# New duration formulas for the kernel's own list scheduler, from the conv taps to the first FFN tiles

## The chip, the core and the metric

The kernel runs on one core of one Trainium2 chip. A core has five engines with queues of their own: TensorE (PE in the profile; its weight loads are listed apart as PEld), VectorE (DVE), ScalarE (ACT), GpSimd (POOL) and SyncE (SP), which here issues the DMA transfers. The metric is device time of one execution in microseconds (us), the median of several runs. Before the change three runs took 810.5, 808.39 and 804.48 us, median 808.39 us.

## The reference, cut to what matters

One decoder layer on 512 tokens of width 1024, in float32:

```python
z = rms_norm(x, mix_norm_g) @ w_in
(q, kc, vc, ks, vs, kw, vw, gl, zg, zc) = split(z)
y_nsa  = nsa_mixer(q, kc, vc, ks, vs, kw, vw, gl, ...)   # 8 heads of 64, 2 kv heads: compressed, selected
                                                        # and window branch, gated and summed
y_gmlp = gelu(u) * (tril(w_s) @ layer_norm(gelu(v)) + b) # width 256, chunks of 128 tokens, 4 groups
y_conv = silu(layer_norm(conv31(a * sigmoid(gate)) + b)) # width 256, causal depthwise, 31 taps
x = x + concat(rms_norm(y_nsa), rms_norm(y_gmlp), rms_norm(y_conv)) @ w_out
x = x + softmax((rms_norm(x) @ wq) @ (rms_norm(mem) @ wk).T / 16) @ (rms_norm(mem) @ wv) @ wo
                                                        # 4 heads of 256, mem has 256 tokens
h = conv3(rms_norm(x) @ w_up)                           # 2 x 2816
x = x + (silu(h[:, :2816]) * h[:, 2816:]) @ w_down
out = rms_norm(x)
```

With 512 tokens, 8 blocks of 64 and N_SELECT 16, the selected branch takes all blocks, and the window of 512 covers all earlier tokens. So both branches are causal attention over the whole sequence with keys and values of their own.

## The kernel before

Every large product is done in split precision. An operand is cut into a high part of type fp32r (on ACT) and the remainder (on DVE or POOL), and `mm3` issues three matmuls into one PSUM tile: high by high, high by low, low by high. Tiles are feature-major, 128 features by 512 tokens, eight k-steps for a sum over 1024.

The program has three stretches. The first norm and the first four column tiles of the input projection are written out by hand, and so is the FFN from its third tile on. All between is put in order, while the program is built, by the class `Lanes`, a list scheduler. Each piece of work is a Python generator (a lane). Before each step it yields the engine of the step, what it reads and which buffers it opens. `Lanes.start` works out when the step could start by a planned clock; `Lanes.run` finds for each engine the lane that can start first, takes among those within a margin EPS of it the most urgent one (smallest number in the table `prio`), and of these picks the earliest over all engines. The planned clock is advanced in `Lanes.account`, which the wrapper `Engine.__getattr__` calls for every instruction: an engine is busy for `cost`, and a reader on another engine may start LAT later, one on the same engine OWN later:

```python
LAT = {"E": 0.18, "S": 0.14, "V": 0.12, "G": 0.14, "D": 0.0}
OWN = {"E": 0.0, "S": 0.05, "V": 0.12, "G": 0.05, "D": 0.0}
```

E, S, V, G and D are TensorE, ScalarE, VectorE, GpSimd and the DMA queue. The plan sets only the order of the instructions in each queue; on the chip each engine takes its queue in order and waits with semaphores. All instructions carry the line of the wrapper, L186, so the rows are told apart by the names of tiles.

The lanes that the prediction speaks of, most urgent first among those that fill:

- `scores` multiplies, for 16 units (token block i of 4, kv head g of 2, branch b of 2; `units` in the order i, g, b), queries by keys of width 128(i+1). `soft` follows: a masked negated maximum per head on DVE (the fused reduce with the mask `cm`, listed as ISA or CUSTOM_DVE_ANT_0), an exponential with its sum on ACT, a reciprocal on DVE, a scaling by the gate on POOL.
- `turns` transposes the probabilities in blocks of 128 on PE, `mix` splits them (ACT, then DVE: tiles tB and tC) and multiplies by the values.
- `taps`: 30 dependent multiply-adds (`scalar_tensor_tensor`) for each of the two conv channel halves, 60 in all, on DVE, with 482 to 511 columns; their weights are the tile `cwh`. Their priority is 7.5, behind almost everything. `conv_post(i)` waits for both halves: two transposes of the accumulators on PE, a layer norm (BN_STATS first), tanh, a norm, and `put_back` into the concatenated y.
- `project` ends with the two halves of the gMLP's product, keys ("u", hf, c); gMLP's tail waits for the second half.
- `mem_work`, the filler of PE: 384 matmuls of 256 columns for keys ("mk") and values ("mv") of the cross-attention memory. `convert` splits its weights on ACT (tile whi) and on POOL (tile wlo, 64 pieces of 256 columns); all other weights are split on ACT and DVE.
- `pow_rstd` gives every norm its reciprocal root: a small operation on DVE and then a power on POOL (tile `nhalf`).
- `tiles("o", ...)`, the mixer's output projection, sums over the eight parts of y in the order in which they come, and ends the attention.

Of the kernel before, what the change touches and what calls it, by code (L numbers as in the profile page):

```python
# [41 lines left out]


class Lanes:
    """Puts the steps of concurrent generators in order: each generator yields the engine of its next step, what the
    step reads and the kinds of slots it opens; the step that can start first goes next, and among those of one
    engine that are about as early, the most urgent one."""

    LAT = {"E": 0.18, "S": 0.14, "V": 0.12, "G": 0.14, "D": 0.0}
    OWN = {"E": 0.0, "S": 0.05, "V": 0.12, "G": 0.05, "D": 0.0}  # L50
# [14 lines left out]
    def account(self, eng, name, a, k):  # L65
        args = list(a) + list(k.values())
        outs = [k["out"] if "out" in k else a[0]] + ([k["accum_out"]] if "accum_out" in k else [])
        aps = [x for x in args if isinstance(x, bass.AP)]
        n = max(int(np.prod(x.shape[1:])) for x in aps)
        if eng == "E":  # L70
            n = int(np.prod((a[2] if name == "matmul" else a[0]).shape[1:]))
            cost = max(int(np.prod(a[1].shape[1:])) / 1200, n / 2400)
        elif eng == "S":
            cost = 0.095 + n / 1200 + 0.093 * ("accum_out" in k)
            table = {AF.Gelu_apprx_tanh: 1, AF.Exp: 2, AF.Silu: 3}.get(a[2], self.table)
            if table != self.table:
                self.table = table
                cost += 1.28
        elif eng == "V":
            cost = (0.13 if name == "scalar_tensor_tensor" else 0.068) + n / 960  # L80
        elif eng == "G":
            cost = 0.245 + n / 1200 * (1 if name == "tensor_scalar" else 2)
        else:
            cost = 0.1 + n / 700
        start = max([self.free[eng]] + [self.at(eng, x) for x in aps] +
                    [self.rd.get(x.tensor.name, 0.0) for x in outs])
        if eng == "E":
            while start >= self.tick + self.TICK:
                self.warm = self.cols >= 3060
                self.cols, self.tick = 0.0, self.tick + self.TICK  # L90
            self.cols += n if name == "matmul" else 256
            cost *= 1 if self.warm else 2
        end = start + cost
        self.free[eng] = end
        if eng == "D":
            end += 2.0
        for x in aps if eng != "D" else ():
            self.rd[x.tensor.name] = max(self.rd.get(x.tensor.name, 0.0), end)
        for x in outs:
            self.wr[x.tensor.name] = (end, eng)  # L100
# [89 lines left out]
def body(ctx, tc, xT, memT, memN, cmask, cmaskT, w_a, w_v, w_u, w_c1, gains, smalls, ws_t, bcs, w_o, w_q, w_k, w_vm,  # L190
# [20 lines left out]
    def slab(shape=(P, T), dt=F32R):  # L211
        return psl.tile(list(shape), dt, name=nm("sl"), tag="slab", bufs=NSLAB)

    def tmp(tag, shape=(P, T), dt=F32):
        return ln.open(tag, pt.tile(list(shape), dt, name=nm("t" + tag), tag=tag, bufs=TB[tag]))
# [7 lines left out]
    def col(n):  # L223
        return pt.tile([P, n], F32, name=nm("rc"), tag="rcol", bufs=4)

    def ps(tag):
        return ln.open(tag, pp.tile([P, T], F32, name=nm("ps"), tag="bank", bufs=8))
# [12 lines left out]
    def mm3(o, ah, al, bh, bl, start, stop):  # L240
        E.matmul(o, ah, bh, start=start, stop=False)
        E.matmul(o, ah, bl, start=False, stop=False)
        E.matmul(o, al, bh, start=False, stop=stop)
# [10 lines left out]
        for _ in gen:  # L254
            pass

    # weight stream
    specs = [(("a", m), w_a[m], (8, 128)) for m in range(12)]
    specs += [(("c1", i), w_c1[i], (16, 64)) for i in range(2)]
    specs += [(("v", c), w_v[:, k0:k1, :], (k1 - k0, 280)) for c, (k0, k1) in enumerate(((0, 3), (3, 6), (6, 8)))]  # L260
# [9 lines left out]
    order = {s[0]: n for n, s in enumerate(specs)}  # L270
# [32 lines left out]
    def ahead(key, n=2):  # L303
        prep(order[key] + n)

    # constants
    gn = pc.tile([P, NGAIN], F32, name="gn")
    sm = pc.tile([P, NSMALL], F32, name="sm")
    cm = pc.tile([P, T], F32, name="cm")
# [1 line left out]
    def gv(name):  # L311
        a, b = GAIN[name]
        return gn[:, a:b]

    def sv(name):
        a, b = SMALL[name]
        return sm[:, a:b]
# [24 lines left out]
    class Norm:  # L342
        def __init__(self, gname):
            self.g = gv(gname)
            self.h = []
            self.acc = None
# [22 lines left out]
            mm3(o[:, :width], wh[:, k, :], wl[:, k, :], hi, lo, first and n == 0, last and n == len(ks) - 1)  # L369
            yield  # L370

    # start: first norm and the first two column tiles side by side
    n1 = Norm("g_mix")
    x = [slab(dt=F32) for _ in range(KD)]
    # wake the activation table and the tensor engine's clock while the first loads run
    wz = tmp("A")
    V.memset(wz, 0.0)
    S.activation(tiny([P, 4]), wz[:, 0:4], AF.Copy)
# [70 lines left out]
    wsr = slab(dt=F32)  # L449
    load(wsr, ws_t)  # L450

    # from here on lanes
    for tag, n in list(PB.items()) + list(TB.items()) + [("raw", NRAW), ("whi", NW), ("wlo", NW), ("bank", 8)]:
        ln.slots[tag] = [0.0] * n
    for o, tag in zip(zc, ("mm", "mm", "s", "s")):
# [14 lines left out]
    def pr(kind, j=0):  # L470
        return prio[kind][j]
# [32 lines left out]
    def spent(key):  # L504
        ln.done(*ready.pop(key))

    # depthwise convolution
    cw = pc.tile([P, 62], F32, name="cwh")
    V.tensor_scalar(cw, sv("cw"), 0.5, None, op0=ALU.mult)
    conv_acc = [slab(dt=F32) for _ in range(2)]  # L510
# [28 lines left out]
                                   op0=ALU.mult, op1=ALU.add)  # L539
        ln.mark(("taps", c), acc)  # L540

    # projection tiles
    qs, kh_, kl_ = {}, {}, {}

    def ev_cmp(kv, o):
# [139 lines left out]
                ln.add(pr("ev", 4), ev_u(hf, i, o))  # L685
        ln.mark("projected")

    # compressed blocks: second layer and scores of all tokens
    w2 = pc.tile([64, 2, 192], F32R, name="w2s")
    split(w2[:, 0, :], w2[:, 1, :], sv("w2")[0:64, :])  # L690
    vcz, kcz, sct = [], [], []
# [64 lines left out]
        for i in range(NT):  # L756
            ln.add(pr("cmp", i), compressed(i))

    # memory: statistics and parts, then keys and values as filler
    rm_col = col(2)  # L760
    rm_bc = pt.tile([P, MEM], F32, name="rm_bc", tag="rmbc", bufs=1)
    g_m = gv("g_m")
# [86 lines left out]
                ln.add(pr("memev", 1), mem_ev("mv", 2 * c + mt, o))  # L849
        ln.mark("quiet")  # L850

    # token-major tails of the gMLP and convolution groups
    g_out = gv("g_out")
    y_hi, y_lo = [None] * KD, [None] * KD
    gx = []
# [121 lines left out]
        yield from put_back(y, 6, i)  # L977
        ln.done(y)

    # native sparse attention  # L980
    units = [(i, g, b) for i in range(NT) for g in range(2) for b in range(2)]
    probs, left = {}, {}
    cmp_p, yts = {}, {}
# [187 lines left out]
                                   y_hi[kt][:, isl].bitcast(F32), op0=ALU.mult, op1=ALU.subtract)  # L1171
        ln.mark(("yn", i), *y_lo[:4])

    # projections of the residual stream
    def tiles(name, parts, deps, after, phases):
        """The first two tiles side by side, phase by phase of their sums, then one tile after the other."""
        o, count = {}, KD if name != "up" else 2
        jobs = [(m, k) for ks in phases for m in range(2) for k in ks]
        jobs += [(m, k) for m in range(2, count) for ks in phases for k in ks]
        first, last = phases[0][0], phases[-1][-1]  # L1180
        for m, k in jobs:
            key = (name, m)
            yield "E", [("w",) + key] + deps(k), ["mm"] if k == first else []
            if k == first:
                o[m] = ps("mm")
            wh, wl = ready[key]
            mm3(o[m], wh[:, k, :], wl[:, k, :], parts[0][k], parts[1][k], k == first, k == last)
            if k == last:
                spent(key)
                ln.add(pr("resid", ("o", "q", "ox", "up").index(name)), after(m, o[m]))  # L1190
# [39 lines left out]
        ln.done(o)  # L1230
        yield from pow_rstd(out_t, tot, 1.0 / D)

    # cross-attention
    n2, n3 = Norm("g_x"), Norm("g_f")
    rx, sc_col = col(NT), col(NT)
    xs, kp, vp = {}, {}, {}
# [108 lines left out]
        oh[k], ol[k] = hi, lo  # L1345
        ln.mark(("oh", k), hi, lo)

    # gated convolutional FFN
    rf = col(NT)
    rf_bc = pt.tile([P, T], F32, name="rf_bc", tag="rbc", bufs=1)  # L1350
    pending = []
# [12 lines left out]
        return iter(())  # L1364

    class Pairs:
        """The parts of a norm's tiles as two lists."""
        def __init__(self, norm, j):
            self.norm, self.j = norm, j

# [29 lines left out]
    lists = lambda norm: (Pairs(norm, 0), Pairs(norm, 1))  # L1400
# [12 lines left out]
    x = xs8  # L1413
    st_ = {}

    # gated convolutional FFN
    fw, fb = sv("fw"), sv("fb")
    ah, al = [], []
    st_["late"] = []
# [45 lines left out]
            split(ah[-1], al[-1], tv)  # L1465
            yield

    # down projection and final norm
    gfin = gv("g_fin")
    acc4 = pt.tile([P, T], F32, name="acc4", tag="acc", bufs=1)  # L1470

# [35 lines left out]
    for m in range(KD):  # L1507
        cuts = (slice(0, T),) if m < KD - 1 else (slice(0, 256), slice(256, T))
        ws_ = []
        for ci, cs in enumerate(cuts):  # L1510
# [4 lines left out]
            for c in range(3):  # L1515
# [3 lines left out]
                for kk in range(8 if c < 2 else 6):  # L1519
                    k = 8 * c + kk  # L1520
# [114 lines left out]
```

## Time and profile before

| what | before |
|---|---|
| runs | 810.5, 808.39, 804.48 us; median 808.39 us |
| span of the profiled execution (the page gives no other time of it) | 801.6 us |
| mean granted TensorE clock | 0.987 |
| busy PE / DVE / ACT / POOL | 785.8 / 532.5 / 393.8 / 128.0 us |
| matmuls and transposes on PE | 4024 |

The span runs from the first to the last instruction of one profiled execution; the runs' times were taken apart from it. Matmuls are pipelined, so that a matmul's listed duration overlaps the next one. What one costs in a dense stretch is read from the distance between starts.

### The profile page before, as it was taken

How to read it: one execution, taken by the hardware profiler on the slowest of the kernel's cores; microseconds unless marked ns; L12 is line 12 of the kernel's file. 1: busy time of each engine (PE TensorE's matmuls, PEld its weight loads, DVE VectorE, ACT ScalarE, POOL GpSimd, SP SyncE). 2: the span in 40 equal slices, each digit the busy share in tenths (PEclk: the TensorE clock that was granted, in tenths of full speed). 3: DMA queues.
4: the chain of work that ended last, by engine and by line, in shares of the span. 5: the costliest groups of instructions: out<-in, count | busy, mean ns of one | idle time of the engine just before them, and what ended most of it. 6: DMA issues, size and time to landing. Idle time of an engine off the chain costs nothing.

```text
span 801.6 us, 10865 instructions
## 1 busy us (share of the span) xinstructions
PE 785.8 (98%) x4024; PEld 657.1 (82%) x4024; DVE 532.5 (66%) x1014; ACT 393.8 (49%) x787; POOL 128.0 (16%) x182
## 2 busy tenths in 40 slices
PE   8999999999999999999999999999999999999995
PEld 6888988878778888888888888888888888888884
DVE  7799857979878865555564787777766767332333
ACT  7455657586677753545442554444443344232221
POOL 0000046647978200100000000000000000000002
PEclk9999989989999999999999999999999999999998
DMA  8522500210222532211032323222222222433303
GB/s 277 183 100 86 182 1 26 82 53 28 105 84 102 202 113 105 79 53 53 32 127 79 105 105 105 82 103 106 86 98 105 91 87 72 125 92 99 99 20 105
DMA packets 26644, 76.96 MB, mean 96 GB/s; under 512 B 2912, under 2 KB 7008, under 8 KB 26592
## 3 DMA queue, kind: packets, MB, share of 16 engines
q1 hardware_dynamic: 26048, 75.76, 27.7%
q8 instruction: 31, 0.51, 0.3%
q10 hardware_dynamic: 544, 0.52, 0.2%
q14 instruction: 21, 0.17, 0.1%
HBM read 74.17 MB, written 2.10 MB: 95 GB/s over the span
## 4 chain that ended last, share of the span: by engine, by line
PE 90%; POOL 4%; DVE 2%; ACT 2%; issue 1%; SPq 1%; DMA 1%; DVEq 0%; POOLq 0%
PE ps L186 90%; POOL wlo L186 2%; POOL ty L186 1%; SPq L186 1%; DMA sl<-in_xT 1%; POOL tpr L186 1%; ACT sl L186 0%; DVE tpr L186 0%; DVE sl L186 0%; ACT whi L186 0%; ACT tpr L186 0%; DVE wlo L186 0%; ACT tD L186 0%; DVE ty L186 0%; DVE tA L186 0%
## 5 line engine op out<-in xcount | busy, mean ns | idle before, releaser
L186 PE MATMUL ps<-sl,whi 128*128 128x512 f32 (+1 forms) x1804 | 531.9, 378 | 0.9 <-DVE sl L186 0.6
L186 PEld LDWEIGHTS ps<-sl,whi 128*128 128x128 f32 x1804 | 331.2, 189 | 64.2 <-DVE sl L186 1.1
L186 PE MATMUL ps<-sl,wlo 128*128 128x512 f32 (+1 forms) x902 | 340.0, 377 | 0.5 <-DVE wlo L186 0.5
L186 ACT ACTIVATE whi<-raw 128x512 fp32r<-128x512 f32 (+4 forms) x227 | 147.4, 673 | 172.6 <-PE ps L186 143.8
L186 PEld LDWEIGHTS ps<-sl,wlo 128*128 128x128 f32 x902 | 170.0, 188 | 31.9 <-DVE wlo L186 0.9
L186 DVE TENSOR_TENSOR wlo<-raw,whi 128x512 fp32r<-128x512 f32 (+5 forms) x163 | 141.2, 878 | 75.9 <-ACT whi L186 69.3
L186 POOL TENSOR_TENSOR ty<-ty,nhalf 128x1 f32<-128x1 f32 (+1 forms) x22 | 13.4, 616 | 365.7 <-DVE ty L186 365.7
L186 DVE TENSOR_TENSOR sl<-ps,sl 128x512 f32<-128x512 f32 (+3 forms) x45 | 29.6, 659 | 61.3 <-PE ps L186 47.9
L186 PE MATMUL ps<-whi,sl 128*128 128x256 f32 (+1 forms) x320 | 65.7, 295 | 0.0
L186 PE MATMUL ps<-sl,sl 128*128 128x256 f32 (+3 forms) x252 | 63.8, 355 | 0.6 <-DVE sl L186 0.6
L186 POOL TENSOR_TENSOR wlo<-raw,whi 128x256 fp32r<-128x256 f32 x64 | 55.5, 889 | 12.6 <-ACT whi L186 12.6
L186 DVE TENSOR_TENSOR tA<-ps,rf_bc 128x512 f32<-128x512 f32 x44 | 30.3, 688 | 40.7 <-PE ps L186 40.7
L186 PEld LDWEIGHTS ps<-sl,sl 128*128 128x128 f32 x252 | 41.5, 193 | 17.3 <-issue 9.4
L186 PEld LDWEIGHTS ps<-whi,sl 128*128 128x128 f32 x320 | 52.7, 194 | 1.6 <-issue 0.5
L186 POOL TENSOR_SCALAR tpr<-tpr,ty,gate 128x128 f32<-128x128 f32 (+3 forms) x64 | 43.5, 688 | 25.7 <-DVE ty L186 14.6
L186 DVE SCALAR_TENSOR_TENSOR sl<-sl,cwh,sl 128x511 f32<-128x511 f32 (+29 forms) x60 | 47.0, 812 | 0.2
L186 PE MATMUL ps<-wlo,sl 128*128 128x256 f32 (+1 forms) x160 | 46.1, 288 | 0.0
L186 ACT ACTIVATE tpr<-tpr,ty 128x128 f32<-128x128 f32 (+3 forms) x64 | 35.4, 554 | 6.9 <-DVE ty L186 6.8
L186 ACT ACTIVATE tB<-ps 128x512 fp32r<-128x512 f32 x48 | 27.8, 593 | 20.6 <-PE ps L186 20.4
L186 DVE CUSTOM_DVE_ANT_0 tpr<-ps,cm 128x128 f32<-128x128 f32 (+3 forms) x64 | 29.6, 480 | 11.6 <-PE ps L186 11.6
L186 DVE TENSOR_TENSOR tC<-ps,tB 128x512 fp32r<-128x512 f32 x48 | 32.0, 681 | 7.6 <-ACT tB L186 7.6
L186 ACT ACTIVATE tD<-sl 128x512 f32<-128x512 f32 (+1 forms) x33 | 19.0, 583 | 34.3 <-DVE sl L186 33.0
(141 smaller groups left out, 729.5 us busy)
## 6 DMA issues: line engine op xcount, KB each, us to landing
raw<-in_w_up SPq DMA_DIRECT2D x44, 512.0 KB, 3.2
raw<-in_w_dn SPq DMA_DIRECT2D x16, 512.0 KB, 3.5
raw<-in_w_a SPq DMA_DIRECT2D x10, 512.0 KB, 3.9
sl<-in_xT SPq DMA_DIRECT2D x16, 256.0 KB, 4.6
raw<-in_w_k SPq DMA_DIRECT2D x8, 512.0 KB, 3.2
raw<-in_w_vm SPq DMA_DIRECT2D x8, 512.0 KB, 3.7
raw<-in_w_o SPq DMA_DIRECT2D x8, 512.0 KB, 3.2
raw<-in_w_q SPq DMA_DIRECT2D x8, 512.0 KB, 3.2
```

The lines of the kernel that those rows point to most:

```text
L186: return fn(*a, **k)
```

## The change

Four formulas of `Lanes.account` are replaced. The latencies LAT and OWN, the margins EPS, the planner's model of the TensorE clock, the table `prio` and all lanes stay. The rest of the diff blanks comments and docstrings.

```diff
         if eng == "E":
             n = int(np.prod((a[2] if name == "matmul" else a[0]).shape[1:]))
-            cost = max(int(np.prod(a[1].shape[1:])) / 1200, n / 2400)
+            cost = max(int(np.prod(a[1].shape[1:])) / 1200, (n + 32) / 2400)
         elif eng == "S":
-            cost = 0.095 + n / 1200 + 0.093 * ("accum_out" in k)
+            cost = 0.19 + n / 1200 + 0.19 * ("accum_out" in k)
...
         elif eng == "V":
-            cost = (0.13 if name == "scalar_tensor_tensor" else 0.068) + n / 960
+            cost = {"scalar_tensor_tensor": 0.21, "tensor_tensor_reduce": 0.22}.get(name, 0.15) + n / 960
         elif eng == "G":
-            cost = 0.245 + n / 1200 * (1 if name == "tensor_scalar" else 2)
+            cost = 0.3 + n / 1200 * (1.5 if name == "tensor_scalar" else 2.7)
```

The instructions and their sizes are the same before and after, 4024 on PE in both. Only their order in the queues differs, from about the 147th instruction of PE to the third tile of the output projection. Three places are shown. In the first two, sl_343 and sl_344 are the two conv accumulators; a row with sm at the left of 128x128 is a transpose.

DVE, the end of the conv taps, before. The ISA rows with `cm` are score reduces, the rows with `cwh` taps, BN_STATS opens `conv_post`:

```order
L186 ISA tpr_2786,ty_2640<-ps_2785,cm 128x512
L186 ISA ty_2640 128x1
L186 TENSOR_TENSOR tC_2767<-ps_2765,tB_2766 128x512
L186 SCALAR_TENSOR_TENSOR sl_344<-sl_470,cwh,sl_344 128x483
L186 RECIPROCAL ty_2846<-ty_2641 128x1
L186 RECIPROCAL ty_2852<-ty_2641 128x1
L186 SCALAR_TENSOR_TENSOR sl_344<-sl_470,cwh,sl_344 128x482
L186 BN_STATS ty_2879<-ps_2870 128x6
```

The last four score reduces come behind these rows. The same place after the change:

```order
L186 SCALAR_TENSOR_TENSOR sl_344<-sl_477,cwh,sl_344 128x485
L186 SCALAR_TENSOR_TENSOR sl_2600<-sl_1684,gn,sl_2599 128x128
L186 SCALAR_TENSOR_TENSOR sl_344<-sl_477,cwh,sl_344 128x484
L186 SCALAR_TENSOR_TENSOR sl_2612<-sl_1684,gn,sl_2611 128x128
L186 SCALAR_TENSOR_TENSOR sl_344<-sl_477,cwh,sl_344 128x483
L186 TENSOR_TENSOR sl_2634<-sl_2634,ps_3305 128x512
L186 SCALAR_TENSOR_TENSOR sl_344<-sl_477,cwh,sl_344 128x482
L186 BN_STATS ty_3323<-ps_3315 128x6
```

Here the last score reduce stands 108 rows above the last tap, and 30 of the 60 taps lie between them; before, none did. The rows between the taps are the norms of the attention's last token blocks (sl_1684, sl_2634).

PE, the first transposes of `conv_post`, before. The 256-column rows with whi and wlo are the memory filler, the rows with tB and tC the attention's products by the values:

```order
L186 MATMUL ps_2826<-wlo_2644,sl_2141 128x256
L186 MATMUL ps_2826<-whi_2643,sl_2142 128x256
L186 MATMUL ps_2870<-sm,sl_343 128x128
L186 MATMUL ps_2870<-sm,sl_344 128x128
L186 MATMUL ps_2874<-sm,sl_343 128x128
L186 MATMUL ps_2874<-sm,sl_344 128x128
L186 MATMUL ps_2647<-tB_2723,sl_1056 128x512
L186 MATMUL ps_2647<-tC_2724,sl_1056 128x512
L186 MATMUL ps_2888<-sm,tpr_2559 128x128
```

The last score matmul of the program follows some 45 rows below. The same place after:

```order
L186 MATMUL ps_3283<-wlo_3187,sl_2451 128x256
L186 MATMUL ps_3283<-whi_3186,sl_2452 128x256
L186 MATMUL ps_3305<-sm,ty_3211 128x128
L186 MATMUL ps_3315<-sm,sl_343 128x128
L186 MATMUL ps_3315<-sm,sl_344 128x128
L186 MATMUL ps_3319<-sm,sl_343 128x128
L186 MATMUL ps_3319<-sm,sl_344 128x128
L186 MATMUL ps_3283<-whi_3267,sl_2524 128x256
L186 MATMUL ps_3283<-wlo_3268,sl_2524 128x256
```

After the change the last score matmul is 345 instructions above these transposes: 300 filler matmuls of 256 columns, 14 matmuls of 512 and 31 transposes lie between. 372 of the 384 filler matmuls come after the last score matmul; before, 144 did. The second half of the gMLP's product has moved from the second token block's turns to between the scores of the fourth.

POOL, the splits of the filler's weights (wlo) and the powers of the norms (nhalf) behind the attention, after:

```order
L186 TENSOR_TENSOR wlo_2971<-raw_2908,whi_2970 128x256
L186 TENSOR_TENSOR wlo_3001<-raw_2948,whi_3000 128x256 x2
L186 TENSOR_TENSOR ty_3073<-ty_3089,nhalf 128x1
L186 TENSOR_TENSOR ty_3084<-ty_3108,nhalf 128x1
L186 TENSOR_TENSOR ty_3098<-ty_3110,nhalf 128x1
L186 TENSOR_TENSOR wlo_3134<-raw_3007,whi_3133 128x256
L186 TENSOR_TENSOR ty_3107<-ty_3162,nhalf 128x1
L186 TENSOR_TENSOR wlo_3134<-raw_3007,whi_3133 128x256 x2
```

48 of the 64 wlo pieces are in the stretch between the last score reduce and the last tap or behind it, with some ten powers among them. Before, most of the pieces stood between the gate scalings of the attention.

## Rows read from the trace of the kernel before

**Rows 1.** The page: span, busy time of each engine, chain of waits by engine.

```profile
span 801.6 us, 10865 instructions
...
PE 785.8 (98%) x4024; PEld 657.1 (82%) x4024; DVE 532.5 (66%) x1014; ACT 393.8 (49%) x787; POOL 128.0 (16%) x182
...
PE 90%; POOL 4%; DVE 2%; ACT 2%; issue 1%; SPq 1%; DMA 1%; DVEq 0%; POOLq 0%
```

**Rows 2.** Windows: stretch, length, busy (instructions) by engine, granted clock, DMA share, GB/s.

```profile
85.00:280.00 195.00, 191.84 (x1200) 161.16 (x1200) 159.22 (x461) 134.23 (x382) 113.06 (x153) 0.96 0.25 84
101.40:108.30 6.90, 6.90 (x26) 5.86 (x27) 4.13 (x26) 3.72 (x17) 2.77 (x6) 0.51 0.00 0
169.70:176.60 6.90, 6.62 (x24) 5.19 (x24) 4.66 (x16) 4.24 (x13) 3.88 (x6) 0.51 0.01 2
176.60:230.00 53.40, 52.38 (x340) 43.01 (x339) 46.80 (x115) 35.34 (x97) 42.57 (x52) 1.00 0.22 75
480.00:500.00 20.00, 20.00 (x90) 16.55 (x89) 15.59 (x20) 9.36 (x12) 0.00 (x0) 1.00 0.29 98
```

**Rows 3.** Timeline of PE near 166 us: start, length, instruction, count, [idle, releaser].

```profile
165.09 0.60 PE L186 MATMUL ps<-sm,tpr 128*128 128x128 f32 x4
165.44 0.79 PE L186 MATMUL ps<-sl,sl 128*128 128x384 f32 x2
166.80 1.56 PE L186 MATMUL ps<-sl,sl 128*128 128x384 f32 x4 [0.57 <-DVE sl L186]
168.29 0.97 PE L186 MATMUL ps<-sm,sl 128*128 128x128 f32 x6
169.36 0.39 PE L186 MATMUL ps<-sl,whi 128*128 128x256 f32 x1
170.03 0.58 PE L186 MATMUL ps<-sl,whi 128*128 128x256 f32 x1 [0.28 <-DVE sl L186]
```

**Rows 4.** Timeline of PE, the memory filler at 140 us.

```profile
140.07 0.28 PE L186 MATMUL ps<-wlo,sl 128*128 128x256 f32 x1
140.19 0.40 PE L186 MATMUL ps<-whi,sl 128*128 128x256 f32 x2
```

**Rows 5.** Waits of PE in the whole span: tile, releaser, idle us, how often, longest.

```profile
PE ps L186 <- DVE sl L186: 3.1, 4, 1.9
```

**Rows 6.** Timeline of DVE at 199 us.

```profile
199.30 0.68 DVE L186 TENSOR_TENSOR tC<-ps,tB 128x512 fp32r<-128x512 f32 x1
199.91 0.67 DVE L186 CUSTOM_DVE_ANT_0 tpr<-ps,cm 128x512 f32<-128x512 f32 x1
```

**Rows 7.** Timeline of ACT at 172 us.

```profile
172.05 0.60 ACT L186 ACTIVATE tpr<-tpr,ty 128x384 f32<-128x384 f32 x1
172.55 0.19 ACT L186 ACTIVATION_READ_ACCUMULATOR tpr<-tpr,ty 128x1 f32 x1
172.64 0.60 ACT L186 ACTIVATE tpr<-tpr,ty 128x384 f32<-128x384 f32 x1
```

**Rows 8.** Timeline of DVE: four conv taps in a row, one beside POOL, the last one.

```profile
144.49 2.65 DVE L186 SCALAR_TENSOR_TENSOR sl<-sl,cwh,sl 128x502 f32<-128x502 f32 x4
...
195.38 1.14 DVE L186 SCALAR_TENSOR_TENSOR sl<-sl,cwh,sl 128x496 f32<-128x496 f32 x1
...
227.82 0.71 DVE L186 SCALAR_TENSOR_TENSOR sl<-sl,cwh,sl 128x482 f32<-128x482 f32 x1
231.53 0.43 DVE L186 BATCH_NORM_STATS2 ty<-ps 128x6 f32<-128x256 f32 x1 [3.00 <-PE ps L186]
```

**Rows 9.** POOL's groups in 101 to 280 us: busy, mean ns of one, idle before.

```profile
L186 POOL TENSOR_TENSOR wlo<-raw,whi 128x256 fp32r<-128x256 f32 x64 | 55.5, 889 | 12.6 <-ACT whi L186 12.6
L186 POOL TENSOR_TENSOR ty<-ty,nhalf 128x1 f32<-128x1 f32 x20 | 12.0, 608 | 12.4 <-DVE ty L186 12.4
```

**Rows 10.** Tile wlo on POOL: shortest, median and longest of the 64 pieces in ns.

```profile
L186 POOL TENSOR_TENSOR wlo<-raw,whi x64: 722/744/3382, 133.6 to 265.1; 128x256 fp32r<-128x256 f32 x64
```

**Rows 11.** Window of the conv taps alone: stretch, length, DVE and ACT busy, clock.

```profile
186.00:230.00 44.00, 14.11 (x15) 0.00 (x0) 1.00 0.25 84
```

## The prediction, made before the changed kernel had run

> **What bounds the kernel now.** I read the page first: PE is busy 785.8 of 801.6 us, and the chain of waits runs through PE for 90% [rows 1]. So almost any time is PE's time, and a new order can win only where PE works slower than it could, or lose where it newly waits. Matmuls and their number are the same. The profiled span is 801.6 us, 6.8 below the median 808.4 of the runs; I make the sum on the span and add 6.8. The changed order covers about 85 to 280 us, where PE issues 1200 of its 4024 instructions [rows 2].
>
> Next the windows of that stretch. Idle time of PE there is only 195.00 - 191.84 = 3.2 us [rows 2]. The clock shows more: in two stretches of 6.9 us the granted clock is 0.51, which is 1.2 in place of 2.4 GHz [rows 2]. At most 6.9 x 0.49 = 3.4 us are lost in each. The second begins right behind the waits near 166 us: PE stands 0.57 us for DVE, and then takes from 168.29 to 170.03 for six transposes and one matmul of 256 columns [rows 3]. Four transposes start 0.35 us ahead of what follows them (165.09 to 165.44), 0.09 each; a filler matmul of 256 columns starts 0.12 after the one before it [rows 3, 4]. Seven instructions that take 6 x 0.09 + 0.12 = 0.66 took 1.74, and of that loss of 1.1 us only 0.28 is listed as idle. So the 0.85 us of idle there stand for 1.7 lost, and I take that factor of 2 for the other waits too. Such waits are for DVE mostly, 3.1 us in four of them [rows 5].
>
> **What the new formulas say.** They are the lengths of the rows. A subtraction of 512 columns is listed with 0.68 us, and the new formula gives 0.15 + 0.53 = 0.68; but the next instruction of DVE starts 0.61 later, which is the old formula, 0.068 + 0.53 = 0.60 [rows 6]. On ACT 0.60 is listed for 384 columns, and what follows starts 0.50 later, with 0.09 more for the accumulator: old 0.51, new 0.70 with the sum's 0.19 [rows 7]. Four taps take 2.65 us in all, about 0.65 each from start to start, while one is listed with 0.71 [rows 8]: old 0.65, new 0.73. So for S and V the plan moves away from the rate at which the engines take instructions, by 0.08 to 0.19 us each, and as LAT stays, the overlapped end is counted twice. For PE the new formula is nearer: (256 + 32)/2400 = 0.12 [rows 4]. For POOL's split it gives 0.30 + 0.58 = 0.88, the mean of 0.889 but not the median of 0.744 [rows 9, 10].
>
> The Trainium skill says the same in "Perfetto Trace Analysis", section "Optimizing Scalar/DVE Operations": the latency that a profile lists holds about twice the fixed overhead, since the half for the acknowledged write overlaps the next instruction. It speaks against planning an engine's rate with listed durations; the rows above agree. By that rule alone the new plan has only the losses below and none of the gains, an estimate of 801.6 + 15.0 + 6.8 = 823.4 us.
>
> **The change part by part.** The plan now believes DVE and ACT fuller than they are. What is least urgent on DVE, the taps, is picked only when nothing else is ready, so half of them fall behind the last score reduce; and what feeds the softmax is believed late, so scores are started early and the filler is left for the end. That is what the two queues show.
>
> *Gains.* (1) The place near 166 us is broken up: 1.7 us of waits and 3.4 of clock, 5.1. (2) The first slow stretch (101 to 108 us) begins at the same early scores, of which little moved: half of 3.4, 1.7, between 0 and 3.4. (3) Of the other waits 3.2 - 0.85 = 2.3 us of idle are left, doubled 4.6; I take 4.2, since PE has more scores in hand. Together 11.0.
>
> *Losses.* (4) The tail. After the last score matmul PE has 300 x 0.12 + 14 x 0.22 + 31 x 0.09 = 41.9 us of work before the first transposes of `conv_post` (0.22 is 20 us by 90 matmuls of 512 columns [rows 2]). DVE has between its last reduce and its last tap, by the old formulas that the spacings confirmed: 30 taps x 0.65 = 19.5; 9 operations of 512 columns x 0.60 = 5.4; 8 of 256 x 0.335 = 2.7; 4 x 0.335 = 1.3; 8 of 128 x 0.20 = 1.6; multiply-adds, 20 of 128 columns x 0.26 = 5.3, 16 of 64 x 0.20 = 3.2, 6 of 256 x 0.40 = 2.4; and 14 tiny ones, some 1.3. Sum 42.7, hardly more than PE's. But in that stretch POOL splits the filler's weights, and taps beside such work are slower: 15 taps in 186 to 230 us took 14.11, 0.94 each [rows 11], with DVE busy 46.8 and POOL 42.6 of 53.4 us in about that window [rows 2]. Against 0.73 listed when alone that is 0.21 more, 30 x 0.21 = 6.3; the ends are 0, and 30 x (1.14 - 0.72) = 12.6 from the slowest kind [rows 8]. I take the middle one, a mean over just this mixture. Other operations with both inputs in SBUF get 1.5. By the same prices the last stretch of scores holds 15.5 us of DVE's work against 12.5 of PE's, so DVE enters the tail late by 0 to 3; I take 1.5. So 42.7 + 6.3 + 1.5 + 1.5 = 52.0 against 41.9: PE waits 10.1 us for the last tap. Before, it was DVE that waited 3.00 for PE there [rows 8]. Behind the first BN_STATS 72 filler matmuls (8.6 us) are left to cover the chain of norms to the last `put_back`, which needs two POOL powers of 0.61 [rows 9] with DVE and ACT steps between; I add 1.5. Tail 11.6. (5) The attention itself is denser, with little filler between score and turn: one new wait of the size of that near 166, 1.7. (6) The clock: a wait of 10 us in the tail may bring one more stretch at 1.2 GHz, 3.4 at an even chance, 1.7. Together 15.0.
>
> What else moves: POOL's powers wait for a DVE that is late, and stand ahead of the next wlo pieces, so the filler's weights come late with it; that is inside (4), since PE waits at the same place and not twice. Each freed weight buffer lets the SP queue load the next one; DMA is busy 22 to 25% there [rows 2], so I cost this at nothing; without that cover a load ahead of the filler would be seen as a wait on whi. The gMLP's tail is moved later by the second half of its product, and lies beside the filler.
>
> Net 15.0 - 11.0 = +4.0: span 805.6, time **812.4 us**. With the contention at its ends, 0 or twice as much (and the 1.5 with it), this case gives 804.6 to 819.
>
> **The rivals.** *DVE and POOL exclude one another* (slower). The longest wlo piece took 3382 ns where the median is 744 [rows 10], and the page shows POOL in 4% of the chain [rows 1], so the two engines do hold each other up. If one stands fully while the other works: 41 pieces of the tail x 0.72 = 29.5 us, taps and other operations with two SBUF inputs 26.5, one after the other 56; with 1.5 of delay 57.5 against 41.9, a wait of 15.6, and the slow clock surely follows (3.4). Losses 15.6 + 1.5 + 1.7 + 3.4 = 22.2, net +11.2, 819.6; up to 827 if half of DVE's other 16 us can't lie beside POOL. It decides once a tap in the tail costs over 1.0 us. Against it: the mean of 0.94 in a stretch where POOL was busy four fifths of the time [rows 2, 11]. The Trainium skill states this rule in "SBUF — State Buffer", section "Who interferes with whom": a DVE instruction with two SBUF inputs and a GpSimd instruction that reads SBUF lock each other out. The long piece agrees, the mean tap only in part. Chance 0.30.
>
> *No contention* (faster). If POOL's pieces lie where DVE reads PSUM, a tap stays at 0.65, DVE's tail is 42.7 + 1.5 and PE waits 2.3; no slow stretch follows, and the first one goes too. Losses 2.3 + 1.7 = 4.0, gains 12.7: net -8.7, 799.7, give or take 2. The point is a tail that DVE ends within 3 us of PE. For it: taps at 0.65 before [rows 8]. Against: 41 pieces in a tail of 42 us. Chance 0.15.
>
> *Nothing* (808): PE is full in any order and the places balance. Chance 0.05, since the queues differ plainly.
>
> **The numbers.** The forecast has 0.50, the slower rival 0.30, the faster 0.15, nothing 0.05. A change under 1%, 800.3 to 816.5, can't be told from none. The forecast's case puts some 0.08 above and 0.02 below that band, the slower rival 0.25 above, the faster one 0.10 below: faster 0.12, same 0.55, slower 0.33. The range 798 to 826 leaves out the faster half of the third case and the end of the second, under 0.15.
>
> **What would show it.** Right: one long wait of PE, about 10 us, for DVE's accumulator right ahead of the first `conv_post` transposes; no slow clock at 170; taps in the tail near 0.94; BN_STATS straight behind the last tap, without the 3.00 of before. Slower rival: taps over 1.0 and wlo pieces over 1 us there, and a clock of 0.5 behind the wait. Faster: taps near 0.7 and a wait under 3. Wrong altogether: PE waiting elsewhere, as in front of scores for ACT or POOL, or the FFN's stretch changing, where the order is the same.

## The result, and the profile after

| | before | after |
|---|---|---|
| median of the runs, us | 808.63 | 830.5 |
| ratio, 95% interval | | 1.0305 [1.0263, 1.0348] |
| profiled span, us | 801.6 | 828.0 |
| mean granted clock | 0.987 | 0.979 |

The changed kernel is slower by 3.05%. The forecast was 812.4 us with a range up to 826: the sign of the net sum was right, its size was not, and the time lies outside the range. Some executions run slower as a whole, at a lower clock, and are left out of comparisons; of the latency cut below this leaves the runs of 823.58 and 833.75 us.

The page of the changed kernel, the lines that answer to [rows 1], and the clock by fortieths of the span:

```profile
span 828.0 us, 10890 instructions
...
PE 795.0 (96%) x4024; PEld 662.1 (80%) x4024; DVE 541.7 (65%) x1014; ACT 394.9 (48%) x787; POOL 128.5 (16%) x182
...
PEclk9999999999898899999999999999999999999997
...
PE 88%; DVE 5%; POOL 2%; DMA 2%; ACT 1%; issue 1%; SPq 1%; DVEq 0%; POOLq 0%
```

DVE's share of the chain has risen from 2 to 5%. The waits of TensorE, answering to [rows 5] (tile, releaser: us, times, longest):

```profile
PE ps L186 <- DVE sl L186: 13.2, 9, 7.3
PE ps L186 <- POOL ty L186: 4.2, 2, 2.7
PE ps L186 <- DVE ty L186: 2.0, 3, 0.9
PE ps L186 <- DVE tC L186: 1.4, 2, 0.7
...
PE ps L186 <- POOL wlo L186: 1.2, 1, 1.2
```

Before, the first line was 3.1 us with a longest of 1.9. Windows of the changed kernel, columns as in [rows 2]; 218.9 is the end of the last score reduce, 279.0 that of the last tap:

```profile
85.00:300.00 215.00, 194.52 (x1178) 161.44 (x1178) 170.46 (x466) 134.79 (x383) 113.50 (x153) 0.94 0.21 67
85.00:218.90 133.90, 130.37 (x733) 101.48 (x733) 96.51 (x303) 90.92 (x252) 55.37 (x83) 0.96 0.15 48
106.30:109.70 3.40, 3.40 (x17) 3.05 (x15) 3.26 (x19) 2.70 (x12) 0.59 (x1) 0.51 0.00 0
160.00:200.00 40.00, 40.00 (x237) 30.49 (x237) 30.13 (x82) 29.11 (x68) 19.86 (x25) 1.00 0.10 34
205.30:212.10 6.80, 6.80 (x20) 4.48 (x18) 4.23 (x11) 3.02 (x9) 2.96 (x3) 0.50 0.50 151
218.90:279.00 60.10, 45.61 (x338) 42.99 (x336) 57.78 (x117) 30.86 (x95) 49.07 (x58) 0.93 0.30 97
249.70:256.50 6.80, 5.55 (x26) 5.26 (x25) 5.59 (x21) 2.22 (x10) 6.80 (x9) 0.50 0.27 81
277.00:283.80 6.80, 4.72 (x22) 4.72 (x23) 5.95 (x17) 2.72 (x8) 1.95 (x4) 0.50 0.25 81
290.70:294.10 3.40, 3.40 (x19) 3.40 (x18) 2.89 (x9) 1.89 (x5) 1.16 (x1) 0.50 0.45 154
```

The same 215 us of the kernel before:

```profile
85.00:300.00 215.00, 211.84 (x1288) 177.71 (x1288) 172.28 (x481) 144.46 (x400) 113.06 (x153) 0.97 0.26 88
```

The reader sees two kinds of loss. TensorE's idle time between 85 and 300 us rises from 3.2 to 20.5 us, by 17.3. The time short of full clock, span by (1 - mean clock), rises from 801.6 x 0.013 = 10.4 to 828.0 x 0.021 = 17.4, by 7.0. Together 24.3 of the 26.4 us by which the span grew. Most of it is in the tail: 60.1 us in which TensorE is idle for 14.5 while DVE is busy 57.8.

The place itself, on TensorE (start, length, instruction, [idle, releaser]):

```profile
265.17 0.66 PE L186 MATMUL ps<-sm,sl 128*128 128x128 f32 x4 [1.33 <-DVE sl L186]
...
279.08 0.90 PE L186 MATMUL ps<-sm,sl 128*128 128x128 f32 x3 [7.29 <-DVE sl L186]
```

and on DVE, answering to [rows 8]:

```profile
273.42 1.18 DVE L186 SCALAR_TENSOR_TENSOR sl<-sl,cwh,sl 128x485 f32<-128x485 f32 x1
274.53 0.81 DVE L186 SCALAR_TENSOR_TENSOR sl<-sl,gn,sl 128x128 fp32r<-128x128 f32 x1
275.26 1.18 DVE L186 SCALAR_TENSOR_TENSOR sl<-sl,cwh,sl 128x484 f32<-128x484 f32 x1
...
278.31 0.71 DVE L186 SCALAR_TENSOR_TENSOR sl<-sl,cwh,sl 128x482 f32<-128x482 f32 x1
279.59 0.43 DVE L186 BATCH_NORM_STATS2 ty<-ps 128x6 f32<-128x256 f32 x1 [0.57 <-PE ps L186]
```

TensorE waits 7.29 us for the last tap. BN_STATS starts 0.57 us after the tap's end, where it had waited 3.00 us for TensorE before. The 14.5 us of idle time in the tail are thus not one wait: besides these 7.29 there are 2.7 us for a power of POOL, 1.2 for a wlo piece and 1.33 for DVE. DVE's end sets their sum. A tap and the short multiply-add behind it take 1.84 us from start to start (273.42 to 275.26).

### The profile page after: what moved, and what is told of

The parts are those of the page before. It is cut to its first block, busy times and chain, and to the rows that moved or that the text cites. A ratio compares the mean times of both kernels' runs of the same rounds, so it can differ in the third digit from the quotient of the medians.

```text
span 828.0 us, 10890 instructions
## 1 busy us (share of the span) xinstructions
PE 795.0 (96%) x4024; PEld 662.1 (80%) x4024; DVE 541.7 (65%) x1014; ACT 394.9 (48%) x787; POOL 128.5 (16%) x182
## 4 chain that ended last, share of the span: by engine, by line
PE 88%; DVE 5%; POOL 2%; DMA 2%; ACT 1%; issue 1%; SPq 1%; DVEq 0%; POOLq 0%
PE ps L186 88%; DVE sl L186 3%; DMA raw<-in_w_a 1%; POOL wlo L186 1%; POOL ty L186 1%; SPq L186 1%; DVE tpr L186 1%; DVE ty L186 0%; DMA tpr<-in_memT 0%; DVE tA L186 0%; ACT tpr L186 0%; DVE wlo L186 0%; ACT tB L186 0%; ACT sl L186 0%; ACT tD L186 0%
## 5 line engine op out<-in xcount | busy, mean ns | idle before, releaser
L186 POOL TENSOR_TENSOR ty<-ty,nhalf 128x1 f32<-128x1 f32 (+1 forms) x22 | 16.5, 753 | 374.9 <-DVE ty L186 374.9
L186 PE MATMUL ps<-whi,sl 128*128 128x256 f32 (+1 forms) x320 | 70.5, 309 | 0.0
L186 PEld LDWEIGHTS ps<-whi,sl 128*128 128x128 f32 x320 | 56.7, 209 | 1.8 <-issue 1.2
L186 DVE SCALAR_TENSOR_TENSOR sl<-sl,cwh,sl 128x511 f32<-128x511 f32 (+29 forms) x60 | 51.9, 883 | 0.3
L186 PE MATMUL ps<-wlo,sl 128*128 128x256 f32 (+1 forms) x160 | 48.6, 304 | 1.2 <-POOL wlo L186 1.2
L186 DVE SCALAR_TENSOR_TENSOR tC<-tA,sm,tC 128x511 f32<-128x511 f32 (+1 forms) x44 | 32.9, 748 | 3.8 <-ACT tC L186 3.0
```

Of the source, the lines that this page charges most:

```text
L186: return fn(*a, **k)
```

## The experiments

Ratios are against the kernel before, run beside each experiment on the same chip (medians 804 to 807 us); on that scale the change itself stands at 1.0305. Three theories: **1**, VectorE's dearer formula pushes the taps behind the scores, and their tail is the loss; **2**, the priority table was fitted to the one order that the old costs gave, and any other order costs time; **3**, the attention's own new order loses, by ScalarE's or GpSimd's formula.

### Which formula: V alone, and all but V

```diff
-            cost = (0.13 if name == "scalar_tensor_tensor" else 0.068) + n / 960
+            cost = {"scalar_tensor_tensor": 0.21, "tensor_tensor_reduce": 0.22}.get(name, 0.15) + n / 960
```

> Only VectorE's formula is new; E, S and G keep the old ones. By the order 37 of the 60 taps then come behind the last score reduce (0 before, 30 after the change). Theory 1 (VectorE's formula alone pushes the taps behind the scores, and TensorE waits for the last one): slower than before by 2.5 to 5%, 828 to 850 us, with a wait of TensorE of 6 us or more ahead of the first conv transposes. Theory 2 (the priority table fits only the old costs, so that any other set of costs loses): slower by 1 to 3%. Theory 3 (ScalarE's or GpSimd's formula is the cause): within 1% of before.

Measured: 838.65 us, 1.0429 [1.0401, 1.0457], slower than the whole change. Its loss is late, with little in the attention (columns as in [rows 2]):

```profile
120.00:200.00 80.00, 78.77 (x453) 59.43 (x451) 58.89 (x184) 56.13 (x155) 39.38 (x63) 1.00 0.08 24
240.00:320.00 80.00, 54.59 (x315) 46.21 (x315) 64.99 (x142) 35.32 (x103) 42.49 (x50) 0.81 0.34 116
```

The same stretches of the kernel before:

```profile
120.00:200.00 80.00, 79.05 (x494) 65.22 (x494) 68.02 (x183) 56.49 (x150) 48.72 (x63) 0.96 0.15 47
240.00:320.00 80.00, 78.81 (x453) 68.34 (x452) 57.71 (x142) 49.29 (x124) 20.86 (x30) 1.00 0.38 132
```

TensorE is idle 25.4 us of the second stretch, at a clock of 0.81. A single wait of 6 us or more at the conv transposes, as I had expected, is not there: the accumulators are tiles sl, and TensorE's longest wait for any tile sl is 3.0 us. The loss is spread over several waits and the clock. The other run has the other three new formulas and this one old:

> E, G and S are new, VectorE's formula is the old one: the complement of the run before. By the order no tap comes behind the last score reduce, and the first conv transposes stand at instruction 940 of TensorE (1321 before, 1503 after the change). Theory 1: 802 to 814 us, no wait over 3 us for the conv accumulators. Theory 2 (any other costs lose): 818 us or more. Theory 3 (S or G): 820 to 832.

Measured: 824.57 us, 1.0254 [1.022, 1.0288]. Theory 1 in its strong form, that the other formulas are harmless, falls: with no tap behind the scores the three other formulas lose nearly as much. Its trace shows where (columns as in [rows 2]):

```profile
120.00:200.00 80.00, 72.91 (x403) 58.72 (x403) 69.02 (x193) 54.06 (x152) 47.22 (x65) 0.86 0.11 34
132.50:142.70 10.20, 9.91 (x36) 8.34 (x37) 7.75 (x18) 3.89 (x12) 6.96 (x9) 0.50 0.00 1
183.70:200.70 17.00, 14.67 (x53) 10.60 (x52) 14.09 (x52) 13.12 (x37) 8.41 (x13) 0.60 0.11 33
```

TensorE is idle 7.1 of those 80 us (1.0 before), and their clock is 0.86 (0.96 before): most of the loss sits in the attention, not in a tail.

### The late taps

```diff
-        conv=..., taps=(7.5, 7.5, 7.5, 7.5), ...
+        conv=..., taps=(4.3, 4.3, 4.3, 4.3), ...
```

> The changed kernel with the priority of the taps raised from 7.5 to 4.3: all 60 taps come ahead of the first score reduce, the rest of the plan keeps the new formulas. Theory 1 (late taps): the long wait at the conv transposes and the waits of 240 to 290 us go, 806 to 816 us; what is left above 808 is the price of a softmax that starts behind the taps. Theory 3 (the attention's own order and the slow clock cost the time, not the taps): 824 us or more.

Measured: 851.98 us, 1.0595 [1.0567, 1.0623], far outside the 806 to 816 us that I had expected. The taps, all ahead of the first score, delay everything:

```profile
PE ps L186 <- DVE sl L186: 29.5, 7, 21.8
```

```profile
60.80:105.20 44.40, 9.79 (x28) 6.67 (x29) 42.95 (x96) 9.22 (x26) 4.66 (x8) 0.50 0.11 33
```

One wait of 21.8 us, and 44 us at half the clock. This does not tell theory 1 from 3, since it moves the same wait to another place. The next one does, as it keeps the order:

```diff
-            V.scalar_tensor_tensor(*tap, op0=ALU.mult, op1=ALU.add)
+            if j < (24, 8)[c]:
+                V.scalar_tensor_tensor(*tap, op0=ALU.mult, op1=ALU.add)
+            else:
+                ln.account("V", "scalar_tensor_tensor", tap, {})
```

> The changed kernel without the 30 taps that come behind the last score reduce: the planner accounts for them, so the order of all else is the same, but they are not issued (that part of the convolution is left out). Theory 1: TensorE's waits for VectorE in the tail go, 13 to 20 us: 811 to 818 us. If the tail is bound by POOL and the late weights of the filler instead: under 6 us, 824 to 830.

Measured: 813.39 us, 1.0117 [1.0091, 1.0143]. So the 30 late taps cost 1.0305 - 1.0117 = 1.9%, some 15 us; 1.2% is left without them. This bounds the price of their place from above, since the run is spared 28.77 us of DVE's work, which any other order would have to put somewhere. The waits of this run (as above) have no long one for DVE:

```profile
PE ps L186 <- DVE sl L186: 3.7, 5, 1.9
PE ps L186 <- DVE ty L186: 3.6, 3, 1.7
```

Then POOL's share in the tail, with the planned order kept:

```diff
-                G.tensor_sub(lo[:, cs], raw[:, cs], hi[:, cs].bitcast(F32))
+                ln.account("G", "tensor_sub", (lo[:, cs], raw[:, cs], hi[:, cs].bitcast(F32)), {})
+                nc.gpsimd.memset(lo[:, cs].bitcast(F32), 0.0)
```

> The changed kernel with the low parts of the memory weights set to zero on POOL in place of subtracted (that part of the computation is left out): the planner accounts for the subtraction, so the order is that of the change, but POOL neither reads SBUF nor waits for ACT there. If taps are slow through POOL's reads: taps of the tail at 0.72 us in place of about 1.0, and 8 to 16 us less than the changed kernel, 813 to 821. If only the number of late taps counts: under 4 us less, 825 to 830.

Measured: 817.68 us, 1.0157 [1.0119, 1.0196], 1.5% or 12 us less than the change. The pair of a tap and a short operation, which took 1.84 us:

```profile
265.37 0.72 DVE L186 SCALAR_TENSOR_TENSOR sl<-sl,cwh,sl 128x486 f32<-128x486 f32 x1
266.00 0.35 DVE L186 SCALAR_TENSOR_TENSOR sl<-sl,gn,sl 128x128 fp32r<-128x128 f32 x1
266.27 0.72 DVE L186 SCALAR_TENSOR_TENSOR sl<-sl,cwh,sl 128x485 f32<-128x485 f32 x1
```

It takes 0.90 here. The run bounds the contention from above, since POOL's operation is also shorter (312 ns at the median, 766 in the changed kernel) and no longer waits for ACT. The two effects, late taps and POOL's reads, overlap and must not be added.

Last, the taps in their old place under the new costs, and the latency cut by what the formulas had added:

```diff
-        taps=(7.5, 7.5, 7.5, 7.5)
+        taps=(7.5, 7.5, 4.3, 4.3)
```

> The changed kernel with only the priority of taps 16 to 30 of each half raised from 7.5 to 4.3. By the order no tap comes behind the last score reduce, and the first conv transposes (1304) and the last score matmul (1347) stand where they stood before the change (1321 and 1364). If the tail of late taps is the loss: 804 to 814 us. If the new costs lose wherever the taps stand (waits in the attention, slow clock): 816 to 828.

Measured: 821.12 us, 1.0219 [1.0144, 1.0294]. Less than a third of the loss goes, and as the interval overlaps the change's [1.0263, 1.0348], even that is not clear of noise. The place of the taps behind the last score reduce is not the whole cause: with none of them there, the kernel still loses 2.2%.

```diff
-    LAT = {"E": 0.18, "S": 0.14, "V": 0.12, "G": 0.14, "D": 0.0}
-    OWN = {"E": 0.0, "S": 0.05, "V": 0.12, "G": 0.05, "D": 0.0}
+    LAT = {"E": 0.18, "S": 0.045, "V": 0.04, "G": 0.085, "D": 0.0}
+    OWN = {"E": 0.0, "S": 0.0, "V": 0.04, "G": 0.0, "D": 0.0}
```

> The changed kernel with LAT and OWN lowered by what the new formulas have added (V 0.12 to 0.04, S 0.14 to 0.045, G 0.14 to 0.085), so that a hand-over from engine to engine is planned about as before and only the engines' rates are slower. If the end counted twice is the loss: 803 to 813 us. If it is the rates of the plan: by the order 25 taps stay behind the last score reduce, 818 to 832.

Measured: 823.58 and 833.75 us, 1.023 and 1.035 of the kernel before (all four runs: 823.58 to 841.94, median 835.19). No run comes near 803 to 813, so the hand-over planned twice is not the whole loss; two runs so far apart can't tell whether a part of it goes. The other half of the reason that the prediction gave, engines planned slower than they are, stands in this run as it was.

### Does any other order pay

Theory 2 asks for orders that carry no new knowledge.

```diff
-        start = max([self.free[eng]] + ...
+        cost *= 1.01; start = max([self.free[eng]] + ...
```

> All four old formulas multiplied by 1.01, a change of the planned times that says nothing new of any engine; some 220 rows of TensorE's queue still stand elsewhere. Theory 1 (wrong proportions between the engines' costs lose the time): within 1% of before, 798 to 811 us. Theory 2 (the priority table was fitted to one exact order; any other order falls into new waits and slow clock): slower by 1 to 3%, 812 to 828.

Measured: 816.14 us, 1.0116 [1.0059, 1.0174]. By 0.99:

> The same by 0.99. Theory 1: within 1% of before, 798 to 811 us. Theory 2: 812 to 828; by the order 8 taps come behind the last score reduce, so a wait at the conv transposes is possible by theory 2 alone.

Measured: 810.36 us, 1.0066 [1.0026, 1.0107]. One per cent on every cost, and the kernel is slower both ways: both intervals lie above 1, the second time within the 798 to 811 us of theory 1. The single formulas, first TensorE's (`n / 2400` becomes `(n + 32) / 2400`, the rest old):

> Only TensorE's formula is new, the one of the four that comes nearer to the spacing of the rows; 30 taps ahead of the first score reduce (25 before), the conv transposes earlier than before. Theory 1: 798 to 811 us. Theory 2: 812 to 828.

Measured: 822.21 us, 1.0214 [1.0171, 1.0258]. The one formula that came plainly nearer to the spacing of the rows loses 2%. GpSimd's line alone, and ScalarE's line alone, each as in the change:

> Only GpSimd's formula is new; by the order the taps end as before, ahead of the last score reduce. If the place of the taps decides: within 1% of before, 798 to 812 us. If any reordering costs as much as TensorE's formula alone did: 814 to 824.

Measured: 810.39 us, 1.0067 [1.003, 1.0104], with no late tap in its trace and little lost.

> Only ScalarE's formula is new; by the order 3 taps come behind the last score reduce, and the last score matmul at 1227 (1364 before). If the place of the taps decides: 803 to 814 us. If ScalarE's overstated cost puts the softmax in the wrong place: 815 to 826, with waits of TensorE in 120 to 200 us, as the run with E, G and S had them.

Measured: 825.09 us, 1.0249 [1.018, 1.0318]. Its loss is mostly clock: the mean granted clock is 0.967, so the time short of full clock is 826.6 x 0.033 = 27.3 us against 10.4 before.

To separate the fit from the costs, the priority table was shifted by the same random factors under old and new costs:

```diff
+    jog = np.random.RandomState(1)
+    prio = {k: tuple(x * (1 + 0.06 * jog.uniform(-1, 1)) for x in v) for k, v in prio.items()}
```

> The kernel before with every entry of the priority table multiplied by a random factor between 0.94 and 1.06 (first draw). If the table is fitted to one order: 812 to 835 us. If the old costs plan well with about any table: 800 to 811.

> The changed kernel with the same draw. Fit: as far above as its twin with the old costs, within 10 us of it, 812 to 840. Costs: 20 us or more above the twin.

> The kernel before with a second draw of the factors. Fit: 812 to 835 us. Costs: 800 to 811.

> The changed kernel with the second draw. Fit: within 10 us of its twin with the old costs. Costs: 20 us or more above it.

The second draw has seed 3 in place of 1. The last column counts the taps that start behind the last score reduce in the traces.

| table | old costs | new costs | new by old | late taps, old and new |
|---|---|---|---|---|
| as it is | 1 | 1.0305 [1.0263, 1.0348] | 1.0305 | 0, 30 |
| first draw | 1.0194 [1.0142, 1.0246] | 1.0547 [1.048, 1.0615] | 1.035 | 8, 30 |
| second draw | 1.017 [1.0118, 1.0222] | 1.047 [1.0415, 1.0526] | 1.030 | 6, 28 |

A random shift of the table costs 1.7 to 1.9% under the old costs and 1.6 to 2.3% under the new. The new costs lose the same 3.0 to 3.5% under all three tables, 24 to 29 us between the twins. That does not show that the costs lose it apart from the fit: a table within 6% of the fitted one still keeps most of its order, and a table fitted anew to the new costs was not run. What the traces do show is that the three pairs lose it in the same place, the tail. The windows of 215 to 320 us, old and new costs under the table as it is, the first and the second draw (columns as in [rows 2]):

```profile
215.00:320.00 105.00, 103.81 (x607) 88.31 (x606) 77.72 (x193) 66.64 (x170) 41.02 (x56) 1.00 0.35 121
215.00:320.00 105.00, 88.05 (x559) 79.66 (x558) 87.43 (x188) 54.90 (x154) 58.71 (x72) 0.92 0.36 118
215.00:320.00 105.00, 101.93 (x623) 87.90 (x623) 78.13 (x185) 62.06 (x164) 50.87 (x66) 1.00 0.38 126
215.00:320.00 105.00, 81.63 (x475) 68.05 (x474) 80.16 (x189) 52.71 (x147) 54.51 (x66) 0.87 0.27 91
215.00:320.00 105.00, 99.36 (x594) 84.97 (x593) 79.70 (x192) 62.61 (x162) 48.45 (x63) 0.97 0.37 121
215.00:320.00 105.00, 86.47 (x548) 78.41 (x548) 86.99 (x195) 57.00 (x164) 68.66 (x82) 0.87 0.35 115
```

TensorE is idle there for 15.8, 20.3 and 12.9 us more under the new costs, and its clock is lower by 0.08 to 0.13. The last two runs asked whose the loss is, under the first draw with V's formula alone and with the other three:

> First draw of the shifted table, only VectorE's formula new. Its twin with the old costs took 822, with all four new 851. If VectorE's formula is the loss that is not the fit's: 838 to 856. If it is spread over the four: 824 to 836.

> First draw of the shifted table, E, G and S new, VectorE's formula the old one. If VectorE's formula is the loss: 814 to 828, about its twin with the old costs. If it is spread over the four: 832 to 845.

Measured: 848.6 us, 1.0537 [1.0476, 1.0598], and 848.89 us, 1.0531 [1.0484, 1.0579]. Either half alone loses as much as all four (851.46 us); the second lies above both ranges that I had given it. They lose it in different places. V's formula alone puts 33 taps behind the last reduce, and TensorE is idle for 29.8 us between 215 and 320. The other three put none there: 140 to 215 us hold 9.9 us of idle time at a clock of 0.80. The losses of the formulas do not add up, and no single one owns them.

## Why the prediction was wrong, step by step

- **What bounds the kernel** held: TensorE is busy 98% before, and both kinds of loss are its waits and its clock.
- **Gain 1**, the place near 166 us, is right as to the place: between 160 and 200 us TensorE is busy 40.00 of 40.00 us at full clock. But the smaller of its two waits has moved and not gone. At 170.03 a filler product waited 0.28 us for DVE [rows 3], for its row `sl<-tpr,gn,sl`, a part of the memory's norm. The same kind of product now waits for the same kind of row 30 us later:

```profile
200.62 0.39 PE L186 MATMUL ps<-sl,whi 128*128 128x256 f32 x1 [0.26 <-DVE sl L186]
203.24 0.39 PE L186 MATMUL ps<-sl,whi 128*128 128x256 f32 x1 [1.14 <-DVE sl L186]
```

```profile
202.70 0.49 DVE L186 SCALAR_TENSOR_TENSOR sl<-tpr,gn,sl 128x256 fp32r<-128x256 f32 x1
```

  After these and one more wait of 0.7 us, for a tile tC, comes a new stretch at half the clock, 205.3 to 212.1 us, about as long as the one that went. **Gain 2**, the first slow stretch: right, 3.4 us long in place of 6.9.
- **Gain 3** failed. The other waits were to shrink by 4.2 us, with 1.7 of new ones in loss 5. By 218.9 us the changed kernel has been idle for 3.5 us, more than the former one in all of 85 to 300 (3.2). Idle and clock up to there are 3.5 + (3.4 + 6.8)/2 = 8.6; the former kernel lost 3.2 + 6.9 = 10.1 at most in the whole stretch. So of the 9.3 us that gains 1 to 3 less loss 5 came to, 1.5 at most are there (the prediction had doubled the listed waits; these sums don't). I had read a denser order as a better covered one; where nearly all waits were small already, the new order had as many, in other places.
- **Loss 4 and 6, the tail**, were the right mechanism and too small. The taps were right: 30 took 28.77 us, 0.959 each (0.724 in the run in which POOL reads nothing), where I had 0.94. The other operations with two SBUF inputs were not. One group of them, in all of the kernel before and in the tail of the changed one:

```profile
L186 DVE SCALAR_TENSOR_TENSOR sl<-sl,gn,sl 128x128 fp32r<-128x128 f32 x16 | 4.5, 346 | 0.0
```

```profile
L186 DVE SCALAR_TENSOR_TENSOR sl<-sl,gn,sl 128x128 fp32r<-128x128 f32 x12 | 8.2, 720 | 0.0
```

  That is 12 x 0.374 = 4.5 us more, where 1.5 was set for all such work. DVE was idle for 2.3 us, where none was counted. So DVE's tail took 60.1 us in place of 52.0 - 1.5 = 50.5 (the 3.0 us beyond the 1.5 and the 2.3 idle make 5.3 of these 9.6; the rest is not told apart), and TensorE was idle 14.5 there in place of 10.1. The clock, set at 1.7, was the worst sized: three stretches from 249.7 to 294.1 us are 17.0 us at 0.50, 8.5 lost at most. From 218.9 to 300 us idle time and clock come to 17.0 + 8.5 = 25.5 us at most, where the tail and loss 6 had 13.3. These 12.2 and the 7.8 of the gains are 20.0 of the 22.4 us between the net +4.0 of the forecast and the measured +26.4.
- **The rule of "SBUF — State Buffer"** in the Trainium skill (section "Who interferes with whom"), which stood beside the slower rival: the runs agree that POOL's reads slow DVE's two-input operations, but the two don't shut each other out wholly (last section). That rival's own mark, taps over 1.0 us and pieces over 1 us, was not reached on the mean (0.959 and 0.897 in the tail), though the last pairs are over it (1.18). It was nearer in time than the forecast. For contention it had 13.3 us (56 against 42.7), I had 7.8; the run without POOL's reads bounds it at 12.
- **"For S and V the plan moves away"** was the reason, with the end counted twice. For ScalarE's exponential with its sum it hardly holds: the next one starts 0.59 us later (172.05 to 172.64 [rows 7]), between the old 0.51 and the new 0.70. The latency cut stays at 1.023 or more, and TensorE's formula, which moved nearer, lost 2.1%. The estimate of 823.4 us that went with this reason lies nearer than the forecast, since few of the gains came, but nearness of a cost to the rows did not forecast the time of the order planned with it. What the prediction lacked is a case of its own: that table and costs fit each other, and that a reordering without new knowledge (1% on all costs, 6% on the table) costs 0.7 to 1.9% where there are only 3 us of idle time to win. I gave 0.05 to "the places balance" and no chance to this.
- **Two slips of the sum** moved nothing. Of the "300" filler matmuls of the tail 12 are other products of 256 columns, so that 84 and not 72 were left behind BN_STATS. And with the contention twice as large the case ends at 812.4 + 6.3 + 1.5 = 820.2 us, not at 819.

So the step that failed is the sizing: the gains of a denser order, which mostly did not come, and the tail with its slow clock, which cost about twice what was set. Open stays why the formulas' losses don't add up, and whether a table fitted anew to the new costs would win the loss back. V's formula loses by late taps, with the table as it was (37 of them, behind 240 us) and under the first draw; the other three lose in the attention, with none. No run here was faster than the kernel before; the nearest, 0.99 of the old costs and GpSimd's formula alone, are 0.7% slower.

## What to carry to other kernels

When a planner's costs and its priorities stand together in a kernel whose bottleneck is 98% busy, take new costs for a random reordering until a new fit of the priorities shows otherwise: measure first what a change of 1% in all costs does, since that is the noise of the planner. Price a reordering by what is last on the queue of the second busiest engine, include what else slows it there, and add the clock that each new wait of the bottleneck costs, which here was a quarter of the loss. Costs read from a profile should be distances between starts, but even the one formula here that came nearer to these gave no better order by itself.

## What the runs showed of the hardware

DVE and POOL hold each other up, and both pay. In the last microseconds of the tail a tap and a short multiply-add took 1.84 us beside two of POOL's subtractions, and 0.90 beside its memsets, which read nothing. If each stood still while the other works, the pair and two pieces of 0.72 us would need some 2.3 us, an estimate from these rows; so they exclude one another in part. Over the 30 late taps the picture is the same: those with no subtraction beside them took 0.71 to 0.73 us, those fully beside some 0.86 to 1.30. POOL's pieces over the whole kernel, first in the changed one and then in the run without the 30 late taps, where all else has the same order:

```profile
L186 POOL TENSOR_TENSOR wlo<-raw,whi 128x256 fp32r<-128x256 f32 x64 | 54.0, 871 | 7.8 <-ACT whi L186 7.5
```

```profile
L186 POOL TENSOR_TENSOR wlo<-raw,whi 128x256 fp32r<-128x256 f32 x64 | 47.8, 773 | 9.1 <-ACT whi L186 8.4 <-PE ps L186 0.6
```

So a piece takes 98 ns less on the mean without the late taps. The medians of the tile show less of this, 766 ns in the changed kernel beside a longest of 1187; POOL's memsets took 312:

```profile
L186 POOL TENSOR_TENSOR wlo<-raw,whi x64: 722/766/1187, 145.6 to 289.3; 128x256 fp32r<-128x256 f32 x64
```

```profile
L499 POOL MEMSET wlo<- x64: 306/312/449, 147.4 to 279.6; 128x256 f32 x64
```

The slow clock can come with no listed wait ahead of it, and last long. With ScalarE's formula alone:

```profile
95.00:103.80 8.80, 8.80 (x41) 6.63 (x40) 4.97 (x22) 5.14 (x17) 0.00 (x0) 1.00 0.53 187
103.80:127.70 23.90, 23.90 (x82) 18.70 (x81) 9.10 (x50) 7.43 (x32) 7.18 (x15) 0.50 0.00 1
```

TensorE is listed as busy throughout the 8.8 us before the clock fell, among them two groups of eight score products that took 2.01 us each. Then 82 instructions filled 23.9 us at 1.2 GHz; the former kernel's stretch in the same place ended after 6.9 us [rows 2].
